# Two DMA queues instead of one in a hybrid decoder layer

## The chip, the cores and the metric

The kernel runs on one core of a Trainium2 chip. The metric is the device time of one execution in microseconds (us). The core has five engines that run side by side, each in its own order: PE (TensorE, matrix products), DVE (VectorE), ACT (ScalarE), POOL (GpSimd) and SP (SyncE). A transfer between memory (HBM) and the core's SBUF is issued by an instruction of SP, ACT or POOL; each of these issues its instructions in order, and if one of them has to wait (for data, or for a buffer to come free), all behind it wait too. This is what "queue" means below.

## The reference

One layer of a decoder, in float32, over 16 learned meta tokens and 2048 tokens of width 1024:

```python
h = jnp.concatenate([meta, x], axis=1)
for l in range(DEPTH):                       # DEPTH = 1
    u = _rmsnorm(h, mix_norm_g[l])
    p = u @ w_in[l]                          # 1024 -> 1792
    p_pool, p_bval, p_bgate, p_cgate, p_cx = jnp.split(p, splits, axis=-1)
    y_a = _pool_mixer(p_pool, pool_w[l], pool_scale[l])
    y_b = _conformer_conv(p_bval, p_bgate, ...)      # 31-tap causal convolution, layernorm
    y_c = _rglru_branch(p_cgate, p_cx, ...)          # gates, linear recurrence over time
    y = jnp.concatenate([y_a, y_b, y_c], axis=-1)
    h = h + y @ w_out[l]
    u = _rmsnorm(h, mlp_norm_g[l])
    h = h + jnp.square(jax.nn.relu(u @ w_up[l])) @ w_down[l]     # 1024 -> 4096 -> 1024
h = _rmsnorm(h, final_norm_g)
return h[:, N_META:]
```

## The kernel before, in words

**Precision.** Products are made in a reduced float format. Each operand is split into a high part and a low part (`split`, lines 113 and 114: ACT rounds to the high part, DVE subtracts to get the low one), and each product is three matmuls: high times high, high times low, low times high. So every weight tile has to be split before PE can use it, unless its split was stored earlier.

**Chunks and items.** The tokens are worked on in four chunks of 512 (chunk 0 has the 16 meta tokens as well). All of PE's large work is a list of items, made in advance: W (input projection, 14 blocks per chunk), O (output projection, 8 per chunk), U and D (up and down projection of the MLP, in four groups), and B (down projection with fewer products, chunk 3). In chunks 1 to 3 U uses a scheme of Strassen's kind: seven products of half size instead of eight, for which sums of weight blocks are needed. In order, O and W of one chunk stand between D of the chunk before and U of the next: O of chunk 1 follows D of chunk 0, and W of chunk 2 follows that.

**Side work.** Everything else (normalisation, mixers, the loads of activations, sums of weights) is written as Python generators. After each item `pump` advances them by a budget of estimated ns, so their instructions are strewn among the items. A scheduler of the framework then lays down the order on each engine and all waits.

**Weights.** The class `Weights` (from line 270 on) feeds the items in order. Raw tiles (128 x 512) are loaded into six buffers `wr` (line 151, called from `dma`), split into five buffers `wh` of twice the size (`split`), and used by PE. Where a split will be needed again, it is stored to HBM (line 309: `wk` for W, `ok` for O, `uk` for U of chunk 1), and later chunks load the stored split straight into `wh` (line 305) instead of splitting again. A `wh` buffer comes free when PE has used it and, if it is stored, when the store has landed.

**Transfers that the change touches**, all in SP's queue before:

- line 177, `gen_fold`: stores of a folded part of `w_out` (8);
- lines 204 to 214, `gen_sums`: loads of blocks of `w_up` into buffers `s` and `t`, sums on DVE, stores to `sums` (16 units of 4 loads and 4 stores), during chunk 0;
- lines 221 to 229, `gen_dsums`: the same for `w_down`, with a split; its high parts go through the `xr` buffers (12 units of 4 loads and 8 stores), during chunks 1 and 2;
- line 309: stores of splits (28 for W, 16 for O, 64 for U);
- line 468, `gen_x`: loads of the activations of chunks 1 to 3, eight each, through the `xr` buffers; line 483, `gen_late`, eight again for chunk 1;
- line 775, `evac_o`: loads of the old activations that O adds to its product, eight per chunk, also through `xr`; the addition is line 777, and it frees one of four PSUM buffers `pm`;
- line 1020, `gen_final`: stores of the results, eight per chunk 0 to 2 (chunk 3 has its own rule and keeps it).

There are two `xr` buffers for all of lines 228, 468, 483 and 775.

`gen_x` for chunk 2 runs during O of chunk 1, and that for chunk 3 during O of chunk 2, each behind `gen_final` of the chunk two before it: first a column sum on PE (lines 382 and 383, `colsum`) and a reciprocal (line 392), then eight scalings (line 1019) with eight stores, then eight loads with squares and splits (lines 400, 401, 158, 159), then a column sum of their squares.

The loads of raw weights are called with the queue as a default, which the change leaves alone:

```python
def w_raw(src, tag="xr", bufs=2, queue=nc.sync):
```

Of the kernel before, what the change touches and what calls it, by code (L numbers as in the profile page):

```python
# [25 lines left out]
F32 = mybir.dt.float32  # L26
# [8 lines left out]
NCH = 4  # L35
META = 16
W0 = NT + META
# [45 lines left out]
def build(nc, tc, x0, xr, w_in, w_out, w_fold, w_up, w_down, vecs, gates, pools, pws, out):  # L83
# [18 lines left out]
    def t_(tag, cols, bufs, dt=F32):  # L102
        shape = [P] + (list(cols) if isinstance(cols, (list, tuple)) else [cols])
        return sb.tile(shape, dt, name=nm(tag), tag=tag, bufs=bufs)
# [7 lines left out]
    def split(hi, lo, src):  # L112
        A.activation(out=hi, in_=src, func=AF.Copy)  # L113
        V.tensor_tensor(out=lo, in0=src, in1=hi.bitcast(F32), op=ALU.subtract)  # L114
# [18 lines left out]
    for b, (w0, w1) in enumerate(((2, 4), (8, 16))):  # L133
# [8 lines left out]
    d_kept = {  # L142
        (g, v): [dp.tile([P, 2, 512], F32, name=f"dk_{g}_{v}_{q}", tag=f"dk_{g}_{v}_{q}") for q in range(4)]
        for g in range(FG - 1) for v in range(KB // 2)
    }
    sums = [dp.tile([P, 2048], F32, name=f"sums_{u}", tag=f"sums_{u}") for u in range(NU)]

    def w_raw(src, tag="xr", bufs=2, queue=nc.sync):
        n = src.shape[-1]
        t = t_(tag, 512, bufs)[:, :n]  # L150
        queue.dma_start(out=t, in_=src)
        return t
# [13 lines left out]
    def gen_fold():  # L166

        pl, pw = b_tile(), b_tile()
        r1, r2 = w_raw(pools), w_raw(pws)
        split(pl[:, 0, :256], pl[:, 1, :256], r1)  # L170
        split(pw[:, 0, :512], pw[:, 1, :512], r2)
        yield 1300

        def store(ps, k, nh):
            t = t_("s", W0, SBF)[:, :NT]
            A.activation(out=t, in_=ps, func=AF.Copy)
            nc.sync.dma_start(
                out=wo_fold[nh * 4 : nh * 4 + 4, :, k * P : (k + 1) * P].rearrange("j p c -> p j c"),
                in_=t.rearrange("p (j c) -> p j c", j=4),
            )  # L180

        for nh in range(2):
            for b in range(2):
                w = f_tile(w_raw(w_fold[b][:, nh * 512 : nh * 512 + 512]), vc("psc", b))
                ps = ps_back()
                mm3(ps, [(pl[:, 0, b * P : (b + 1) * P], pl[:, 1, b * P : (b + 1) * P], w[:, 0], w[:, 1])])
                store(ps, b, nh)
                yield 750
            pss = [ps_back() for _ in range(2)]
            for j in range(2):  # L190
                w = f_tile(w_raw(w_fold[2 + j][:, nh * 512 : nh * 512 + 512]))
                for i in range(2):
                    m0 = j * 256 + i * P
                    mm3(pss[i], [(pw[:, 0, m0 : m0 + P], pw[:, 1, m0 : m0 + P], w[:, 0], w[:, 1])], j == 0, j == 1)
                yield 700
            for i in range(2):
                store(pss[i], 2 + i, nh)
            yield 0

    def gen_sums(u):  # L200

        a11, a12, a21, a22 = (t_(t, W0, n)[:, :512] for t, n in (("s", SBF), ("t", TB), ("t", TB), ("s", SBF)))
        for t, m, c0 in ((a21, 1, 0), (a22, 1, 512), (a11, 0, 0), (a12, 0, 512)):
            nc.sync.dma_start(out=t, in_=w_up[2 * u + m][:, c0 : c0 + 512])
        yield 0
        V.tensor_tensor(out=a22, in0=a21, in1=a22, op=ALU.add)
        V.tensor_tensor(out=a21, in0=a11, in1=a21, op=ALU.subtract)
        nc.sync.dma_start(out=sums[u][:, 1536:2048], in_=a22)
        nc.sync.dma_start(out=sums[u][:, 1024:1536], in_=a21)
        yield 1400  # L210
        V.tensor_tensor(out=a11, in0=a22, in1=a11, op=ALU.subtract)
        V.tensor_tensor(out=a12, in0=a12, in1=a11, op=ALU.subtract)
        nc.sync.dma_start(out=sums[u][:, 0:512], in_=a11)
        nc.sync.dma_start(out=sums[u][:, 512:1024], in_=a12)
        yield 1400

    def gen_dsums(g, v):

        a11, a12, a21, a22 = (t_(t, W0, n)[:, :512] for t, n in (("s", SBF), ("t", TB), ("t", TB), ("s", SBF)))
        for t, m, c0 in ((a21, 1, 0), (a22, 1, 512), (a11, 0, 0), (a12, 0, 512)):  # L220
            nc.sync.dma_start(out=t, in_=w_down[g, 2 * v + m][:, c0 : c0 + 512])
        yield 0

        def put(q, t):
            hi = t_("xr", NT, 2, F32R)
            A.activation(out=hi, in_=t, func=AF.Copy)
            V.tensor_tensor(out=t, in0=t, in1=hi.bitcast(F32), op=ALU.subtract)
            nc.sync.dma_start(out=d_kept[g, v][q][:, 0], in_=hi.bitcast(F32))
            nc.sync.dma_start(out=d_kept[g, v][q][:, 1], in_=t)

        V.tensor_tensor(out=a22, in0=a21, in1=a22, op=ALU.add)
        V.tensor_tensor(out=a21, in0=a11, in1=a21, op=ALU.subtract)
        yield 1400
        V.tensor_tensor(out=a11, in0=a22, in1=a11, op=ALU.subtract)
        V.tensor_tensor(out=a12, in0=a12, in1=a11, op=ALU.subtract)
        yield 1400
        put(0, a11)
        put(1, a22)
        yield 1400
        put(2, a21)  # L240
        put(3, a12)
        yield 1400
# [37 lines left out]
    class Weights:  # L280
# [17 lines left out]
        def split(self, n):  # L298
            while self.ns < min(n, len(self.srcs)):
                self.dma(self.ns + 1)  # L300
                t = t_("wh", (2, 512), WH, F32R)
                _, keep, kept = self.srcs[self.ns]
                with tc.high_priority(EARLY):
                    if kept is not None:
                        nc.sync.dma_start(out=t.bitcast(F32), in_=kept)
                    else:
                        split(t[:, 0], t[:, 1], self.raw.pop(self.ns))
                if keep is not None:
                    nc.sync.dma_start(out=keep, in_=t.bitcast(F32))
                self.hl[self.ns] = t  # L310
                self.ns += 1

# [95 lines left out]
    for c in range(NCH):  # L408
        o = Chunk()
# [15 lines left out]
    def a_tile():  # L425
        return t_("U", (2, NT), 8, F32R)

    def b_tile():
        return t_("H", (2, W0), HB, F32R)
# [30 lines left out]
    def gen_x(o):  # L460

        o.x = []
        if o.c > 1:
            ss = t_("ss", W0, 2)
        for k in range(KB):
            hl = a_tile()
            raw = t_("xr", NT, 2)
            nc.sync.dma_start(out=raw, in_=xr[o.c - 1, k])
            if o.c > 1:
                add_square(ss, raw, 0, NT, k == 0)  # L470
            split_to(hl[:, 0], hl[:, 1], raw, vc("g1", k))
            o.x.append(hl)
            yield 1300
        if o.c > 1:
            o.rs1 = rsqrt_of([colsum(ss[:, :NT])], subs_of(o), 1.0 / D)
            yield 3500

    def gen_late(o):

        ss = t_("ss", W0, 2)  # L480
        for k in range(KB):
            raw = t_("xr", NT, 2)
            nc.sync.dma_start(out=raw, in_=xr[o.c - 1, k])
            add_square(ss, raw, 0, NT, k == 0)
            yield 620
        o.rs1 = rsqrt_of([colsum(ss[:, :NT])], subs_of(o), 1.0 / D)
        yield 3500
        for kind, i, t in o.held:
            evac_w(o, kind, i, [t])
            yield 700  # L490
# [279 lines left out]
    def evac_o(o, j, ps):  # L770
        if j == 0:
            o.h = []
            o.ss2 = t_("ss", W0, 2)
        raw = t_("xr", NT, 2)
        nc.sync.dma_start(out=raw, in_=(x0[j, :, META:W0] if o.c == 0 else xr[o.c - 1, j]))
        h = htile(o, j)
        V.tensor_tensor(out=h[:, :NT], in0=ps, in1=raw, op=ALU.add)  # L777
        add_square(o.ss2, h[:, :NT], 0, NT, j == 0)
        o.h.append(h)
# [227 lines left out]
    def gen_final(o, s0, s1):  # L1007
        if o.c == NCH - 1:

            ps = ps_back()  # L1010
            for n, t in enumerate((o.ssf, o.sq7)):
                T.matmul(ps[:, : s1 - s0], ones.bitcast(F32), t[:, s0:s1], start=(n == 0), stop=(n == 1))
        else:
            ps = colsum(o.ssf[:, s0:s1])
        rs = rsqrt_of([ps], [(s0, s1)], 1.0 / D)
        yield 3300
        for k in range(KB):
            h = o.h[k][:, s0:s1]
            V.scalar_tensor_tensor(out=h, in0=h, scalar=vc("gf", k), in1=rs[:, s0:s1], op0=ALU.mult, op1=ALU.mult)
            (nc.scalar if o.c == NCH - 1 and k % 2 else nc.sync).dma_start(out=out[o.c, k, :, s0:s1], in_=h)  # L1020
            yield 660


# [113 lines left out]
    for it in items:  # L1137
        kind, c, j, _ = it
# [18 lines left out]
    for n, it in enumerate(items):  # L1157
        kind, c, j, (s0, s1) = it
        o = ch[c]
# [156 lines left out]
```

## Time and profile before

| | |
|---|---|
| Time, median of 3 runs | 2005.56 us (2005.14 to 2010.1) |
| The profiled execution | 2004.47 us |
| Its span, first to last instruction | 2002.6 us |
| Granted clock of PE, mean | 0.991 |
| DMA, all queues | 464.20 MB, mean 232 GB/s |
| q1, SP's queue | 199632 packets, 460.61 MB, 68.4% of 16 engines' span |
| q10, ACT's queue | 1584 packets, 1.64 MB, 0.2% |

The table says that practically all bytes went through SP's queue, and that the 16 DMA engines of the core were busy with it for about two thirds of the span. The profile's page cuts the span into 40 slices and gives a digit for the busy share of each engine, in tenths. The digits of PE are 9 nearly everywhere. An engine that is busy in nearly every slice sets the time, so the places where it is not busy are what one looks for; the waits, in which the profile says what each engine waited for and what ended the wait, tell why. In the lines of these views, `h<-pm,xr` is the output buffer and the inputs, and `SPq L1020` is an instruction that SP issues for line 1020. In the timeline the first number is the start in us from the start of the span, the second the duration, and the bracket tells how long the engine had been idle and what released it.

### The profile page before, as it was taken

To read this page: it belongs to the slowest core of one execution; us is meant where nothing else is said; L and a number is where in the kernel's file an instruction comes from. 1 tells how busy PE (TensorE), PEld (TensorE's weight loads), DVE (VectorE), ACT (ScalarE), POOL (GpSimd) and SP (SyncE) were. 2 spreads that over 40 slices of the span, in tenths; PEclk is the share of its full clock that TensorE was granted. 3 is DMA by queue.
4 is the path that set the end of the run, shared out by engine and by line. 5 is a ranking of instruction groups with operands and counts; after the bars stand their busy time and mean duration, and the time that the engine had idled before them with its cause. 6 is when DMAs were issued, how large, how long until landed. Compare 5 with 4: busy or idle time off the path is not lost.

```text
span 2002.6 us, 30672 instructions
## 1 busy us (share of the span) xinstructions
PE 1933.2 (97%) x11080; PEld 1672.0 (83%) x11080; DVE 1461.2 (73%) x2394; ACT 1016.6 (51%) x1704; POOL 0.2 (0%) x4
## 2 busy tenths in 40 slices
PE   8999999999999899999999889999999998999998
PEld 8778878777887689888888768988888888999998
DVE  7987589966753699569787489856768478676667
ACT  5586364556542326467675231545467435353443
POOL 0000000000000000000000000000000000000000
PEclk9999999999999899999999999999999999999999
DMA  9635756735847579488767759847876638888874
GB/s 319 206 127 192 246 178 197 239 121 180 267 151 246 179 249 320 137 300 282 256 236 258 247 184 307 293 156 271 301 255 212 228 116 281 285 279 283 282 253 153
DMA packets 201368, 464.20 MB, mean 232 GB/s; under 512 B 22144, under 2 KB 28416, under 8 KB 201216
## 3 DMA queue, kind: packets, MB, share of 16 engines
q1 hardware_dynamic: 199632, 460.61, 68.4%
q8 instruction: 87, 1.43, 0.3%
q10 hardware_dynamic: 1584, 1.64, 0.2%
q14 instruction: 65, 0.53, 0.1%
HBM read 353.11 MB, written 109.05 MB: 231 GB/s over the span
## 4 chain that ended last, share of the span: by engine, by line
PE 72%; DMA 12%; DVE 9%; ACT 4%; issue 3%; SPq 1%; ACTq 0%; DVEq 0%
PE pm L331 44%; PE pm L355 10%; PE pw L355 10%; PE pm L345 5%; DMA wh<-uk 3%; DMA xr<-d_xr 2%; DVE wh L114 2%; DVE ca L591 2%; DMA wh<-dk 1%; DMA uk<-wh 1%; ACT wh L113 1%; DMA s<-d_w_up 1%; PE pb L638 1%; DVE fr L870 1%; DMA t<-d_w_up 1%
## 5 line engine op out<-in xcount | busy, mean ns | idle before, releaser
L331 PE MATMUL pm<-U,wh 128*128 128x512 f32 (+1 forms) x3072 | 691.4, 384 | 5.7 <-DVE wh L114 5.5
L331 PEld LDWEIGHTS pm<-U,wh 128*128 128x128 f32 x3072 | 554.1, 188 | 131.5 <-DVE wh L114 6.6
L113 ACT ACTIVATE wh<-wr 128x512 fp32r<-128x512 f32 x576 | 355.4, 626 | 416.0 <-PE pm L331 227.3
L114 DVE TENSOR_TENSOR wh<-wr,wh 128x512 fp32r<-128x512 f32 x576 | 388.3, 687 | 184.3 <-ACT wh L113 180.2
L331 PE MATMUL pm<-H,wh 128*128 128x512 f32 (+1 forms) x2112 | 455.1, 374 | 22.4 <-DVE h L777 15.2
L331 PEld LDWEIGHTS pm<-H,wh 128*128 128x128 f32 x2112 | 373.3, 192 | 99.9 <-DVE h L777 16.9
L355 PE MATMUL pm<-H,wh 128*128 128x256 f32 x2304 | 293.5, 282 | 7.9 <-DMA wh<-uk 7.8
L355 PEld LDWEIGHTS pm<-H,wh 128*128 128x128 f32 x2304 | 282.2, 188 | 12.5 <-DMA wh<-uk 8.0
L355 PE MATMUL pw<-H,wh 128*128 128x256 f32 x1728 | 224.8, 283 | 11.0 <-DVE fr L870 6.6
L355 PEld LDWEIGHTS pw<-H,wh 128*128 128x128 f32 x1728 | 212.1, 189 | 17.2 <-issue 6.9
L345 PE MATMUL pm<-U,wh 128*128 128x512 f32 (+1 forms) x624 | 143.1, 387 | 0.1
L345 PEld LDWEIGHTS pm<-U,wh 128*128 128x128 f32 x624 | 113.2, 188 | 25.7 <-ACT wh L113 1.0
L591 DVE SCALAR_TENSOR_TENSOR ca<-Pbv,vec,ca 128x512 f32<-128x512 f32 x180 | 128.1, 745 | 0.1
L401 DVE TENSOR_TENSOR ss<-ss,fr 128x512 f32<-128x512 f32 (+1 forms) x82 | 53.4, 651 | 64.6 <-ACT fr L400 62.8
L870 DVE TENSOR_TENSOR fr<-pw,fr 128x512 f32<-128x512 f32 x96 | 66.1, 688 | 31.4 <-PE pw L355 29.4
L857 DVE TENSOR_TENSOR U<-fr,U 128x512 fp32r<-128x512 f32 x104 | 71.3, 687 | 21.3 <-ACT fr L856 21.0
L997 DVE TENSOR_TENSOR h<-h,pm 128x512 f32<-128x512 f32 (+1 forms) x100 | 66.8, 670 | 17.0 <-PE pm L331 15.8
L966 ACT ACTIVATE fr<-fr 128x512 f32<-128x512 f32 x48 | 30.2, 629 | 78.0 <-DVE fr L965 78.0
L400 ACT ACTIVATE fr<-h 128x512 f32<-128x512 f32 (+1 forms) x45 | 27.7, 620 | 77.4 <-DVE h L777 52.7
L855 ACT ACTIVATE U<-fr 128x512 fp32r<-128x512 f32 x104 | 64.9, 626 | 1.6
L856 ACT ACTIVATE fr<-fr 128x512 f32<-128x512 f32 x104 | 64.7, 624 | 1.4
L392 DVE RECIPROCAL rs<-rs 128x512 f32<-128x512 f32 (+2 forms) x17 | 53.9, 3169 | 13.5 <-ACT rs L390 13.4
(269 smaller groups left out, 1662.8 us busy)
## 6 DMA issues: line engine op xcount, KB each, us to landing
wr<-d_w_down SPq DMA_DIRECT2D x260, 256.0 KB, 3.6
wh<-uk SPq DMA_DIRECT2D x128, 512.0 KB, 5.2
wr<-d_w_up SPq DMA_DIRECT2D x208, 256.0 KB, 3.5
wh<-wk SPq DMA_DIRECT2D x64, 512.0 KB, 3.9
uk<-wh SPq DMA_DIRECT2D x64, 512.0 KB, 4.9
wh<-ok SPq DMA_DIRECT2D x48, 512.0 KB, 4.2
wh<-dk SPq DMA_DIRECT2D x48, 512.0 KB, 5.1
wr<-sums SPq DMA_DIRECT2D x64, 256.0 KB, 5.9
```

What stands on the lines that cost most here:

```text
L113: A.activation(out=hi, in_=src, func=AF.Copy)
L114: V.tensor_tensor(out=lo, in0=src, in1=hi.bitcast(F32), op=ALU.subtract)
L331: T.matmul(ps[:, : s1 - s0], w_block(w, k, a, paired), rhs[k][:, b, s0:s1], start=(k == 0 and j == 0), stop=(k == KB - 1 and j == 2),)
L345: T.matmul(ps[:, : s1 - s0], w_block(w, k, a, True), rhs[k][:, b, s0:s1], start=(k == 0 and j == 0), stop=(k == KB - 1 and j == 2),)
L355: T.matmul(ps, w[:, a, k * P : (k + 1) * P], op[k][b], start=(k == 0 and j == 0), stop=(k == 3 and j == 2),)
L392: V.reciprocal(rs[:, c0:c1], rs[:, c0:c1])
L591: V.scalar_tensor_tensor(out=a, in0=o.ub[i][:, k : k + NT], scalar=vc("cw", i * CONVK + k), in1=a, op0=ALU.mult, op1=ALU.add)
L855: A.activation(out=f[:, 0], in_=r, func=AF.Square)
L856: A.activation(out=r, in_=r, func=AF.Square)
L857: V.tensor_tensor(out=f[:, 1], in0=r, in1=f[:, 0].bitcast(F32), op=ALU.subtract)
L870: V.tensor_tensor(out=out.rearrange("p (a c) -> p a c", a=2), in0=ps.rearrange("p (a c) -> p a c", a=2), in1=x.unsqueeze(1).broadcast_to([ ...
L997: V.tensor_tensor(out=h, in0=h, in1=ps[:, : s1 - s0], op=ALU.add)
```

## The change

The listed transfers are issued by POOL (`nc.gpsimd`) instead of SP. SP keeps the first loads of the activations of chunk 0, the loads of raw weights and of stored splits, and half of the results of chunk 3; the other half of those stays on ACT. Nothing else changes: sizes, buffers, items and budgets are the same. The diff, without the lines around:

```diff
 gen_fold, store
-            nc.sync.dma_start(
+            nc.gpsimd.dma_start(
                 out=wo_fold[nh * 4 : nh * 4 + 4, :, k * P : (k + 1) * P].rearrange("j p c -> p j c"),
 gen_sums
-            nc.sync.dma_start(out=t, in_=w_up[2 * u + m][:, c0 : c0 + 512])
+            nc.gpsimd.dma_start(out=t, in_=w_up[2 * u + m][:, c0 : c0 + 512])
-        nc.sync.dma_start(out=sums[u][:, 1536:2048], in_=a22)
-        nc.sync.dma_start(out=sums[u][:, 1024:1536], in_=a21)
+        nc.gpsimd.dma_start(out=sums[u][:, 1536:2048], in_=a22)
+        nc.gpsimd.dma_start(out=sums[u][:, 1024:1536], in_=a21)
-        nc.sync.dma_start(out=sums[u][:, 0:512], in_=a11)
-        nc.sync.dma_start(out=sums[u][:, 512:1024], in_=a12)
+        nc.gpsimd.dma_start(out=sums[u][:, 0:512], in_=a11)
+        nc.gpsimd.dma_start(out=sums[u][:, 512:1024], in_=a12)
 gen_dsums
-            nc.sync.dma_start(out=t, in_=w_down[g, 2 * v + m][:, c0 : c0 + 512])
+            nc.gpsimd.dma_start(out=t, in_=w_down[g, 2 * v + m][:, c0 : c0 + 512])
-            nc.sync.dma_start(out=d_kept[g, v][q][:, 0], in_=hi.bitcast(F32))
-            nc.sync.dma_start(out=d_kept[g, v][q][:, 1], in_=t)
+            nc.gpsimd.dma_start(out=d_kept[g, v][q][:, 0], in_=hi.bitcast(F32))
+            nc.gpsimd.dma_start(out=d_kept[g, v][q][:, 1], in_=t)
 Weights.split
-                    nc.sync.dma_start(out=keep, in_=t.bitcast(F32))
+                    nc.gpsimd.dma_start(out=keep, in_=t.bitcast(F32))
 gen_x and gen_late
-            nc.sync.dma_start(out=raw, in_=xr[o.c - 1, k])
+            nc.gpsimd.dma_start(out=raw, in_=xr[o.c - 1, k])
 evac_o
-        nc.sync.dma_start(out=raw, in_=(x0[j, :, META:W0] if o.c == 0 else xr[o.c - 1, j]))
+        nc.gpsimd.dma_start(out=raw, in_=(x0[j, :, META:W0] if o.c == 0 else xr[o.c - 1, j]))
 gen_final
-            (nc.scalar if o.c == NCH - 1 and k % 2 else nc.sync).dma_start(out=out[o.c, k, :, s0:s1], in_=h)
+            ((nc.scalar if k % 2 else nc.sync) if o.c == NCH - 1 else nc.gpsimd).dma_start(out=out[o.c, k, :, s0:s1], in_=h)
```

More of the change, by code (lines that the diff above doesn't have):

```diff
@@ L482, in gen_late @@
             raw = t_("xr", NT, 2)
-            nc.sync.dma_start(out=raw, in_=xr[o.c - 1, k])
+            nc.gpsimd.dma_start(out=raw, in_=xr[o.c - 1, k])
             add_square(ss, raw, 0, NT, k == 0)
```

## The prediction, made before the result was known

> **What bounds the kernel now.** I read the page first, for the engine that fills the span.
>
> ```profile
> span 2002.6 us, 30672 instructions
> PE 1933.2 (97%) x11080; PEld 1672.0 (83%) x11080; DVE 1461.2 (73%) x2394; ACT 1016.6 (51%) x1704; POOL 0.2 (0%) x4
> PE 72%; DMA 12%; DVE 9%; ACT 4%; issue 3%; SPq 1%; ACTq 0%; DVEq 0%
> ```
>
> TensorE (PE) is busy for 1933.2 of 2002.6 us, so about 69 us of holes, and some slow matmuls behind them, are all that a change of transfers alone can win. GpSimd (POOL) does nothing after four start-up instructions. The second view is the list of waits of PE: it names what ended the holes.
>
> ```profile
> PE pm L331 <- DVE h L777: 15.2, 4, 5.9
> PE pb L382 <- ACT hl L113: 9.1, 4, 6.3
> PE pm L355 <- DMA wh<-uk: 7.8, 9, 1.9
> ```
>
> (Columns: total us, times, longest.) L777 is the addition that empties PSUM in the output projection (kind O); it needs the old activations in an `xr` buffer. L382 is the sum over columns, whose place in PE's order is fixed, so everything behind it waits as well. The third line is late weights. Third, the table by stretches, to see where the first two lie.
>
> ```profile
> 650.00:700.00 50.00, 39.89 (x152) 31.03 (x153) 34.01 (x52) 18.27 (x28) 0.00 (x0) 0.86 0.56 180
> 1150.00:1200.00 50.00, 43.77 (x174) 34.03 (x174) 41.23 (x64) 18.90 (x31) 0.00 (x0) 0.91 0.51 174
> ```
>
> After the length of the stretch comes PE's busy time. These two stretches, the projections of chunks 1 and 2, lose 10.1 and 6.2 us, and the granted clock falls to 0.86 and 0.91. The DMA share is only 0.56 and 0.51, so it is not bandwidth that lacks there. Fourth, the waits of the DMA queue on SyncE (SP), which issues in order.
>
> ```profile
> SPq L309 <- DVE wh L114: 150.1, 78, 11.0
> SPq L228 <- ACT xr L226: 31.5, 19, 6.0
> SPq L1020 <- DVE h L1019: 18.6, 7, 15.4
> ```
>
> All three lines are stores for whose data the queue stands still, with weights and activations behind them. These waits go away from SP with the change; most of them cost PE nothing, as DVE and the weights run ahead.
>
> **The first place: output projection of chunk 1.** The queue's view, then the timeline of the engines:
>
> ```profile
> 625.84 0.34 SPq L1020 DMA_DIRECT2D d_out<-h  x1
> 638.20 1.31 SPq L1020 DMA_DIRECT2D d_out<-h  x1
> 640.56 0.33 SPq L305 DMA_DIRECT2D wh<-ok  x1
> 640.98 0.87 SPq L468 DMA_DIRECT2D xr<-d_xr  x2
> ```
>
> ```profile
> 629.71 0.74 DVE L1019 SCALAR_TENSOR_TENSOR h<-h,vec,rs 128x512 f32<-128x512 f32 x1
> 630.97 0.74 DVE L159 SCALAR_TENSOR_TENSOR U<-xr,vec,U 128x512 fp32r<-128x512 f32 x1
> 645.80 0.63 ACT L400 ACTIVATE fr<-xr 128x512 f32<-128x512 f32 x1 [14.08 <-DMA xr<-d_xr]
> 653.31 7.83 PE L331 MATMUL pm<-H,wh 128*128 128x512 f32 x24 [4.42 <-DVE h L777]
> 667.41 0.79 PE L382 MATMUL pb<-hl,ones 128*128 128x512 f32 x1 [6.27 <-ACT hl L113]
> ```
>
> The eight results of chunk 0 (L1020) are ready when DVE ends the last one, 629.71 + 0.74 = 630.45. SP needs from 625.84 to past 638.20 for their stores, because between them stand loads `wh<-ok`, each of which waits until PE has released a weight buffer. Only then, at 640.98, come the next two loads of activations for chunk 2 (L468), though an `xr` buffer was free at 630.97 + 0.74 = 631.71. ACT waits 14.08 us for them. There are two `xr` buffers for eight such loads and for the additions at L777, so from 640.98 to the column sum at 667.41 run four rounds of load and use, 26.4 us. PE idles 4.42 and 6.27 us in it.
>
> With the change the eight stores and these loads stand in POOL's queue, in the same order among themselves, without the weights. Let g be POOL's time to issue one transfer, and d how much later than from SP it lands. Then the pair is issued at the later of 631.71 and 625.84 + 8g instead of 640.98, and the column sum comes 4d later for its four rounds: a change of 8g - 15.1 + 4d.
>
> **The second place: output projection of chunk 2.**
>
> ```profile
> 1116.68 5.38 DVE L1019 SCALAR_TENSOR_TENSOR h<-h,vec,rs 128x512 f32<-128x512 f32 x8
> 1117.65 0.42 SPq L1020 DMA_DIRECT2D d_out<-h  x1
> 1121.97 0.69 DVE L777 TENSOR_TENSOR h<-pm,xr 128x512 f32<-128x512 f32 x1
> 1131.28 0.45 SPq L1020 DMA_DIRECT2D d_out<-h  x1
> 1134.05 0.44 SPq L468 DMA_DIRECT2D xr<-d_xr  x1
> ```
>
> ```profile
> 1147.80 8.03 PE L331 MATMUL pm<-H,wh 128*128 128x512 f32 x24 [5.87 <-DVE h L777]
> 1157.12 0.51 PE L382 MATMUL pb<-hl,ones 128*128 128x512 f32 x1 [1.30 <-ACT hl L113]
> 1163.05 2.50 PE L331 MATMUL pm<-H,wh 128*128 128x512 f32 x5 [4.71 <-DVE h L777]
> ```
>
> The same figure: data ready at 1116.68 + 5.38 = 1122.06, stores from 1117.65, next load at 1134.05; PE idles 5.87 + 1.30 + 4.71 = 11.9 us. The last hole ends behind a fifth round (the addition after the column sum). In POOL's queue the load goes at 1117.65 + 8g, and both buffers are free from 1121.97 + 0.69 = 1122.66. Change: 8g - 16.4 + 5d.
>
> **The third place: results of chunk 2 between the weights of chunk 3.**
>
> ```profile
> 1668.32 1.93 SPq L1020 DMA_DIRECT2D d_out<-h  x2
> 1680.08 0.71 PE L355 MATMUL pm<-H,wh 128*128 128x256 f32 x4 [1.93 <-DMA wh<-uk]
> ```
>
> SP stands 1.93 us at these stores, loads `wh<-uk` behind it, and PE later waits 1.93 us for such a load. I credit that once: -1.9 us. The other late weights of the third line of PE's waits lie where no moved transfer stands ahead of them, or can't be told apart; I credit nothing, and 7.8 - 1.9 = 5.9 us is what it could be at most.
>
> **What POOL's queue adds.** The program moves 476 transfers: 8 of the fold, 16 x 8 of the sums of `w_up`, 12 x 12 of those of `w_down`, 108 stored splits (28 + 16 + 64), 64 loads of activations, 24 results. None of them was issued by POOL in this trace, so g and d have to be bounded. For g: SP's rows above show 0.34 to 0.45 us for an issue; at the other end POOL would issue one only when the one before has landed, 3.4 us:
>
> ```profile
> xr<-d_xr SPq DMA_DIRECT2D x56, 256.0 KB, 3.4
> xr<-d_gates SPq DMA_DIRECT2D x1, 256.0 KB, 2.8
> ```
>
> For d: the same size landed in 2.8 us where little else was queued, so a transfer that no longer queues behind weights may gain 0.6; and it can lose a whole landing, 3.4. In total even 476 x 3.4 = 1618 us fits into the span, so POOL as a whole is not full; only its places count. I take g = 0.8, twice SP's row, as the same 128 rows have to be described, and d = 0.5, near zero for the same DMA engines.
>
> Where d hurts is where a store has to land before its buffer can be used again:
>
> ```profile
> ACT wh L113 <- DMA uk<-wh: 11.7, 8, 2.9
> ACT xr L226 <- DMA dk<-xr: 23.1, 15, 4.5
> ```
>
> ```profile
> 854.26 0.63 ACT L113 ACTIVATE wh<-wr 128x512 fp32r<-128x512 f32 x1 [2.79 <-DMA uk<-wh]
> 863.08 1.67 PE L355 MATMUL pw<-H,wh 128*128 128x256 f32 x12 [2.02 <-DVE fr L870]
> ```
>
> ```profile
> 381.34 11.32 PE L345 MATMUL pm<-U,wh 128*128 128x512 f32 x48
> 386.97 0.82 ACT L623 ACTIVATE t<-Pcx,vec 128x512 f32<-128x512 f32 x1 [2.98 <-DMA sums<-t]
> 397.66 4.62 PE L331 MATMUL pm<-U,wh 128*128 128x512 f32 x12 [3.84 <-DVE wh L114]
> ```
>
> In the U blocks of chunk 1 ACT already waits 8 times for a stored split to leave its `wh` buffer; the wait of 2.79 us at 854.26 is followed by a hole of 2.02 us on PE. I let all eight grow by d and reach PE: 8d. The stores of the sums of `w_up` did the same once (2.98 us of ACT, then 3.84 us of PE); two of them: 2d. The 15 waits for `dk<-xr` I cost at nothing: they lie in the D blocks, where 48 matmuls, two items or four weight tiles, take 11.32 us, so the five tiles prepared ahead cover some 14 us against a longest wait of 4.5; without that cover they would cost another 15d. SP's issue time that falls away lies beside PE's work and is worth nothing by itself.
>
> **The sum.** 8g - 15.1 + 4d, and 8g - 16.4 + 5d, and -1.9, and 10d make 16g + 19d - 33.4. With g = 0.8 and d = 0.5: -6.7, -7.5, -1.9 and +5.0, together -11.1 us. The profiled execution took 2004.47 us (span 2002.6 and 1.9 around it); it becomes 1993.4. The median of the runs before, 2005.56, is 1.1 above the profiled execution, so I forecast 1994.5 us. Late next on PE would still be the column sum, about 6 us earlier than now.
>
> The Trainium skill, page "DMA: Bandwidth & Descriptors", section "Latency and other measured facts", gives about 0.6 us to the first byte from SyncE and about 1 us from GpSimd, where software writes the descriptors; no run here shows it yet. By it d would be 0.4, and the sum, as an estimate, -13.0 instead of -11.1 us.
>
> **Rivals.** *No change.* The change does not do all that it says: the loads of activations still stand behind the eight result stores, only in another queue, and the two `xr` buffers still make four or five rounds in turn. At g = 1.0 and d = 0.9 the sum is 16.0 + 17.1 - 33.4 = -0.3: 2005.3 us. For it speak the rounds in the rows above, against it that d would be a quarter of a whole landing, 0.9 of 3.4. The same page's section "Issuing engines are not separate DMA queues" speaks for it, too: transfers of all queues run on the same DMA engines, and another queue saves only issue time. The trace agrees that bandwidth is not missing in the two stretches (DMA shares 0.56 and 0.51), but what SP loses there is waiting in line, not issue time.
>
> *Slower.* POOL's transfers are dear enough to turn every round and every buffer that a store has to leave into a longer wait. It decides from 16g + 19d = 33.4 on. At g = 1.5 and d = 1.5 the stores take 12 us before the load can go, the two projections end 2.9 and 3.1 us later than now, the stored splits and sums cost 15, and the third place still gives 1.9 back: 24.0 + 28.5 - 33.4 = +19.1, 2024.7 us. For it: ACT's waits of 11.7 us show that the split buffers have no slack in chunk 1. Against it: g there would be four times SP's row.
>
> *Much faster.* g = 0.4 and d = -0.6: the load goes as soon as its buffers are free, and the holes of both projections close, 10.7 + 11.9 us; the 24 matmuls after each, which took 7.83 and 8.03 us where 48 take 11.32, run 2.2 us faster each; with the third place -29 us, 1977 us. Against it: the rounds through two buffers would have to become shorter than PE's work.
>
> **How the numbers follow.** A measurement of this kernel can tell about 0.3%, 6 us, from no change. The sum is faster than that when 16g + 19d is below 27.4 (at g = 0.8, d below 0.77), slower when it is above 39.4 (at g = 0.8, d above 1.4). I give 0.39 to the forecast, 0.08 to much faster, 0.27 to no change and 0.26 to slower: 0.47 faster, 0.27 same, 0.26 slower. The range for 8 in 10 reaches from near the much faster case, 1978, to near the slower one, 2022. By itself the forecast's own range is 1985 to 1999.
>
> **What would show it.** Right: POOL issues of under 1 us; the load L468 after the last L1020 at about 7 us (chunk 1) and 10 us (chunk 2) sooner after the first L1020 than now; PE's wait at L777 nearly gone, that at L382 shorter; clock above 0.9 in those stretches; ACT's waits for `uk<-wh` up by a few us. Wrong: landings from POOL over 1 us later than from SP, more of PE's time waiting for `wh` splits in chunk 1, new holes in the D blocks of chunk 0 behind `sums`, or an order of instructions on PE that moves the column sum to another place, which I have left as it is.

## The result, and the profile after

In the runs on one chip the kernel before took 2005.35 us (median of 4), the kernel after 2102.05 us (median of 4): 1.0468 times as long, 95% interval 1.044 to 1.0497. The profiled execution of after took 2094.55 us, its span is 2092.8. I had forecast 1994.5; the sign was wrong. The top of the page of after:

```profile
span 2092.8 us, 30923 instructions
PE 1959.3 (94%) x11080; PEld 1695.1 (81%) x11080; DVE 1463.3 (70%) x2394; ACT 1014.7 (48%) x1702; POOL 259.6 (12%) x480
...
q1 hardware_dynamic: 128016, 307.49, 45.4%
q0 software_dynamic: 44992, 153.12, 20.2%
```

The change did what it says: 153 MB moved to a queue of POOL (q0), and POOL is busy 12% of the span, with issuing. PE does the same 11080 matmuls. Its holes grew from 69 to 133 us (span less busy time), and the matmuls themselves took 26 us more, at a mean granted clock of 0.976 instead of 0.991. The two prices that the prediction had bounded can be read from the groups and from the landings of after:

```profile
L309 POOL DMA_DIRECT2D uk<-wh x64 | 34.2, 534 | 269.1 <-DVE wh L114 205.8 <-DVE fr L965 62.7 <-issue 0.2
...
uk<-wh POOLq DMA_DIRECT2D x64, 512.0 KB, 5.7
xr<-d_xr POOLq DMA_DIRECT2D x56, 256.0 KB, 4.0
dk<-xr POOLq DMA_DIRECT2D x48, 256.0 KB, 4.5
```

An issue takes 534 ns here and 0.54 us as the mean of all 480 (259.6 us), so g = 0.54, under my 0.8. The landings were 4.9, 3.4 and 3.4 us before: by these medians d is 0.6 to 1.1, say 0.85, over my 0.5. In the formula of the prediction they give 16 x 0.54 + 19 x 0.85 - 33.4 = -8.6 us. (It is -6.4 us if the loads also have to wait for their buffers, free at 631.71 and 1122.66; the formula had left that bound out, which counts at so low a g.) So it isn't the medians of the two prices that failed, but the formula.

The first place, the output projection of chunk 1, in the timeline of after:

```profile
654.92 5.18 POOL L1020 DMA_DIRECT2D d_out<-h  x8 [3.50 <-DVE h L1019]
660.79 1.18 POOL L468 DMA_DIRECT2D xr<-d_xr  x2 [0.69 <-DMA d_out<-h]
668.02 0.63 ACT L400 ACTIVATE fr<-xr 128x512 f32<-128x512 f32 x1 [7.60 <-DMA xr<-d_xr]
678.07 4.44 PE L331 MATMUL pm<-H,wh 128*128 128x512 f32 x18 [0.47 <-DVE h L777]
690.57 0.79 PE L382 MATMUL pb<-hl,ones 128*128 128x512 f32 x1 [8.06 <-ACT hl L113]
```

The loads L468 go 660.79 - 654.92 = 5.9 us after the first result, where it was 640.98 - 625.84 = 15.1. The wait at L777 is down to 0.47 us. The column sum comes 35.7 us after the first result instead of 41.6: 5.9 us won, where the terms of this place, 8g - 15.1 + 4d, give -7.4 at the measured prices, and -5.9 with the bound by the buffer. PE gained less: from the first matmul of this output projection to the first of the next stage it took 57.4 us, 61.0 before, as the wait ahead of the column sum grew from 6.27 to 8.06 us. The second output projection took 56.3 us, 62.4 before. So both places gained. In the table by stretches they lie at 650 to 700 and 1200 to 1250; a third stretch is worse, at the head of the U blocks of chunk 2. The same work had PE busy for 47.92 us (364 matmuls, clock 1.00) in the stretch 1250 to 1300 of before:

```profile
650.00:700.00 50.00, 41.47 (x166) 32.81 (x166) 29.30 (x37) 14.93 (x24) 11.90 (x22) 0.90 0.73 246
...
1200.00:1250.00 50.00, 40.46 (x166) 31.95 (x165) 34.97 (x54) 17.17 (x26) 4.85 (x9) 0.90 0.59 189
1300.00:1350.00 50.00, 38.68 (x264) 36.50 (x263) 42.53 (x68) 15.73 (x28) 7.06 (x13) 0.86 0.77 260
```

So the time is lost elsewhere. The waits of PE say at what:

```profile
PE pw L355 <- DVE fr L870: 36.7, 16, 6.5
PE pb L382 <- ACT hl L113: 20.1, 4, 8.6
PE pm L355 <- DMA wh<-uk: 12.4, 9, 3.9
```

The same wait as in the first line, before:

```profile
PE pw L355 <- DVE fr L870: 6.6, 9, 2.0
```

Here PE waits for DVE to add up the results in `pw`. The second line, the wait at the column sum, which I had expected to be shorter, was 9.1 us before. One of the 16 times of the first line, in a U block of chunk 2, with what DVE and ACT did ahead of it:

```profile
1313.02 2.93 PE L355 MATMUL pm<-H,wh 128*128 128x256 f32 x12 [3.88 <-DMA wh<-uk]
1314.37 0.63 ACT L226 ACTIVATE xr<-t 128x512 fp32r<-128x512 f32 x1 [6.09 <-DMA dk<-xr]
1320.06 3.39 DVE L591 SCALAR_TENSOR_TENSOR ca<-Pbv,vec,ca 128x512 f32<-128x512 f32 x5
1323.97 0.69 DVE L870 TENSOR_TENSOR fr<-pm,q 128x512 f32<-128x512 f32 x1
1327.10 0.69 DVE L870 TENSOR_TENSOR fr<-pw,fr 128x512 f32<-128x512 f32 x1
1327.84 2.93 PE L355 MATMUL pw<-H,wh 128*128 128x256 f32 x12 [6.48 <-DVE fr L870]
```

Two things stand here. ACT waits 6.09 us for a store of a weight sum to land. And DVE, which is not idle, runs seven taps of the convolution (L591) and three splits of weights (L114) in the 7 us before the addition that PE needs, at 1327.10. The taps are this place's own: in all 16 waits together they fill 4.0 of the 36.7 us, splits of weights 12.1, and for 8.3 DVE stands idle until ACT has done its half of a split (L113). What stands ahead of what on DVE is a matter of order: the framework lays the instructions of each engine out by its own model of time, and with another queue it laid them out anew. If one compares the two programs engine by engine and keeps as many instructions as possible that stand in the same order in both, 154 of PE's 11060 are left over, 486 of DVE's 2394 and 211 of ACT's 1655.

### The profile page after: what moved, and what is told of

It is laid out like the page before. It is cut to its first block, busy times and chain, and to the rows that moved or that the text cites. A ratio compares the mean times of both kernels' runs of the same rounds, so it can differ in the third digit from the quotient of the medians.

```text
span 2092.8 us, 30923 instructions
## 1 busy us (share of the span) xinstructions
PE 1959.3 (94%) x11080; PEld 1695.1 (81%) x11080; DVE 1463.3 (70%) x2394; ACT 1014.7 (48%) x1702; POOL 259.6 (12%) x480
## 4 chain that ended last, share of the span: by engine, by line
PE 44%; issue 22%; DMA 16%; DVE 10%; POOL 4%; ACT 3%; POOLq 0%; DVEq 0%; ACTq 0%; SPq 0%
PE pm L331 25%; PE pm L355 7%; PE pw L355 7%; PE pm L345 3%; DMA xr<-d_xr 3%; DVE ca L591 3%; DMA wh<-uk 2%; DMA s<-d_w_up 2%; DMA wh<-dk 2%; DVE wh L114 1%; DMA uk<-wh 1%; POOL uk L309 1%; DMA sums<-s 1%; DMA dk<-t 1%; DMA dk<-xr 1%
## 5 line engine op out<-in xcount | busy, mean ns | idle before, releaser
L113 ACT ACTIVATE wh<-wr 128x512 fp32r<-128x512 f32 x576 | 356.5, 627 | 452.0 <-PE pm L331 244.1
L114 DVE TENSOR_TENSOR wh<-wr,wh 128x512 fp32r<-128x512 f32 x576 | 390.3, 688 | 237.5 <-ACT wh L113 235.1
L331 PEld LDWEIGHTS pm<-H,wh 128*128 128x128 f32 x2112 | 374.8, 193 | 91.8 <-ACT wh L113 7.2
L355 PE MATMUL pm<-H,wh 128*128 128x256 f32 x2304 | 301.6, 287 | 14.4 <-DMA wh<-uk 12.4
L355 PEld LDWEIGHTS pm<-H,wh 128*128 128x128 f32 x2304 | 291.0, 194 | 19.1 <-DMA wh<-uk 11.8
L355 PE MATMUL pw<-H,wh 128*128 128x256 f32 x1728 | 235.3, 291 | 50.6 <-DVE fr L870 36.7
L355 PEld LDWEIGHTS pw<-H,wh 128*128 128x128 f32 x1728 | 221.1, 196 | 58.4 <-issue 29.2
L591 DVE SCALAR_TENSOR_TENSOR ca<-Pbv,vec,ca 128x512 f32<-128x512 f32 x180 | 128.5, 750 | 0.1
L870 DVE TENSOR_TENSOR fr<-pw,fr 128x512 f32<-128x512 f32 x96 | 66.1, 688 | 28.2 <-PE pw L355 26.4
L309 POOL DMA_DIRECT2D uk<-wh x64 | 34.2, 534 | 269.1 <-DVE wh L114 205.8
```

What stands on the lines that cost most here:

```text
L309: nc.gpsimd.dma_start(out=keep, in_=t.bitcast(F32))
L331: T.matmul(ps[:, : s1 - s0], w_block(w, k, a, paired), rhs[k][:, b, s0:s1], start=(k == 0 and j == 0), stop=(k == KB - 1 and j == 2),)
L355: T.matmul(ps, w[:, a, k * P : (k + 1) * P], op[k][b], start=(k == 0 and j == 0), stop=(k == 3 and j == 2),)
L591: V.scalar_tensor_tensor(out=a, in0=o.ub[i][:, k : k + NT], scalar=vc("cw", i * CONVK + k), in1=a, op0=ALU.mult, op1=ALU.add)
L870: V.tensor_tensor(out=out.rearrange("p (a c) -> p a c", a=2), in0=ps.rearrange("p (a c) -> p a c", a=2), in1=x.unsqueeze(1).broadcast_to([ ...
```

## The experiments

**Theories.** *Order*: the new order of PE, DVE and ACT costs the time, whatever the queue. *Transfer*: what POOL issues lands later, and buffers and engines wait for it. To part them I held the order. A table for each engine lists one kernel's instructions in their order, and each instruction gets an edge to the one before it that binds the order of issue alone:

```diff
+    for text in ORDERS.values():
+        ...
+            tc.add_manual_dep(
+                ins, prev.name,
+                mybir.DependencyInfo(mybir.DependencyClass.NoSync, mybir.DependencyReason.DATA),
```

The kernel before, held to its own order in this way, is the same program, instruction for instruction, so the edges add nothing. "Old order" below means that PE, DVE, ACT and SP are held to the order of before. The tables shift the line numbers: by 75 in the kernels at old order, by 86 in the two with small writes.

**Order and queue apart.** `e1`: the diff of the change, at the old order. `e2`: before, with PE, DVE and ACT held to the order of after.

> All moved transfers are issued by POOL as in the changed kernel, but the order of instructions on PE, DVE, ACT, SP and (among the moved ones) POOL is pinned to that of the kernel before, by edges that order issue only. Theory 'order' (the framework's scheduler, which works with its own model of time, laid down another order on DVE, ACT and PE because the queue changed, and that order costs the 90 us): the loss is gone, about 1997 us (the sum of the prediction with the measured issue of 0.54 us and 0.85 us later landing: -8.6), at any rate 1985 to 2015. Theory 'transfer' (POOL's transfers land later and stand in one line, so buffers of splits and sums come free later): as slow as the changed kernel, 2080 to 2105.

> All transfers stay in SP's queue as before, but the order of instructions on PE, DVE and ACT is pinned to that of the changed kernel. Theory 'order': as slow as the changed kernel, 2070 to 2110. Theory 'transfer': like the kernel before, 2000 to 2015.

| kernel | queue | order | median, us | to before (95%) |
|---|---|---|---|---|
| after | POOL | new | 2102.05 | 1.0468 (1.044 to 1.0497) |
| `e1` | POOL | old | 2054.04 | 1.0247 (1.0215 to 1.028) |
| `e2` | SP | new | 2109.46 | 1.0532 (1.05 to 1.0565) |

The kernel before took 2002.75 us beside `e1` and `e2`. Neither theory is alone. The transfers cost 51 us without a change of order, and on top of them the new order costs 48 us (after against `e1`). The order of after costs 107 us even without a single transfer moved. The two don't add: at the new order the POOL queue is no worse than SP's. Part of the 107 us is a mismatch, as a place of `e2` shows (its line numbers are 59 higher than before's: L290 is L231, L929 is L870):

```profile
1528.07 0.69 DVE L290 TENSOR_TENSOR s<-t,s 128x512 f32<-128x512 f32 x1 [10.99 <-DMA s<-d_w_down]
1528.68 0.68 DVE L929 TENSOR_TENSOR fr<-pw,fr 128x512 f32<-128x512 f32 x1
1529.42 4.44 PE L414 MATMUL pw<-H,wh 128*128 128x256 f32 x24 [6.44 <-DVE fr L929]
```

DVE stands idle for 10.99 us until blocks of `w_down` have landed for a weight sum, and the addition that PE needs stands behind. Its waits for these blocks are 69 us in all, 14 before and 22 in after. So this order suits loads that don't stand in line behind weights, and the price of the order in after itself is the 48 us.

**The groups of transfers, order free and held.** The edit is the diff of the change, for the lines named alone: activations and results (468, 483, 775, 1020), stored splits (309), sums and fold (177, 204 to 229).

> Only the loads of activations (lines 468, 483, 775) and the results (line 1020) go to POOL; stored splits, sums and the fold stay on SP; the scheduler is free. Theory 'transfer': the terms for stored splits and sums fall away, and the two output projections gain as in the prediction, 16 x 0.54 + 9 x 0.85 - 33.4 = -17, 1988 us (1980 to 2000). Theory 'order': the order changes here too, so part of the loss stays although no stored split is on POOL, 2010 to 2070.

> Only the stores of splits (line 309) go to POOL, the scheduler is free. Theory 'transfer': these stores hold the weight buffers of chunk 1 longer, where the changed kernel lost some 30 us in the U blocks of chunk 1, so 2020 to 2045. Theory 'order': the loss follows what the scheduler does with the order, not the buffers; waits of ACT for these stores stay near the 11.7 us of before, and holes of PE end at DVE instead.

> Only the weight sums and the fold (lines 177, 204 to 229) in GpSimd's queue, the order laid anew. If 'order' and 'transfer' add, the transfers give what this group gives at the old order (next run, about 1.018) and the order something between 0 and 25 us more: 1.018 to 1.030. If the new order happens to suit, no more than 1.018.

> Order of the engines that of the kernel before; only lines 468, 483, 775 and 1020 (activations and results of the last norm) in GpSimd's queue. With all but the splits it was 42 us slower at this order. Theory 'sums' (those 42 us belong to the weight sums and their results: store, landing, next use of the same two buffers xr and of t, with ScalarE standing in line): 0.993 to 1.000 here, the gains at the heads of chunks 1 and 2 alone. Theory 'any transfer from GpSimd' (each group pays for landing later): 1.005 to 1.012, the gains eaten.

> Order of the engines that of the kernel before; of the transfers only the stored splits (line 309) go to GpSimd's queue, all others stay in SyncE's. Theory 'split buffer' (what is left of the loss at the old order, some 50 us, is that the five buffers of the weight splits are given back later, because each store is issued and lands later from GpSimd: 34 us of ScalarE's waits for uk<-wh, 11.7 before): 1.015 to 1.025 of the time before, with those waits at 25 us or more. Theory 'sums and results' (the loss sits with the sums of chunk 2, whose results land later, 33.9 us of waits for dk<-xr against 23.1): 1.000 to 1.005.

> The same group at the order of before. All but the splits cost 42 us at this order and the activations 5 of them: 1.016 to 1.021, with the place of 12 us in the D stage of chunk 2. If the groups only hurt together (activations and sums in one line on GpSimd), under 1.010.

> Order of the engines that of the kernel before; all of the change except line 309: activations, results, sums and fold in GpSimd's queue, stored splits in SyncE's. 'Split buffer': 0.994 to 1.003, the place of 15 us in the D stage of chunk 2 gone or nearly so, and the gain at the heads of chunks 1 and 2 kept (2 to 5 us each). 'Sums and results': 1.015 to 1.025, with the place in chunk 2 still there.

| moved to POOL | order free | old order |
|---|---|---|
| activations, results | `e3` 1.0027 (1.0008 to 1.0046) | `e10` 1.0024 (1.0003 to 1.0045) |
| stored splits | `e4` 1.0221 (1.0187 to 1.0255) | `e6` 1.0109 (1.0088 to 1.0131) |
| sums, fold | `e5` 1.0325 (1.03 to 1.0351) | `e17` 1.0211 (1.0171 to 1.0251) |
| all but the splits | | `e7` 1.02 (1.0157 to 1.0243) |
| all | after 1.0468 | `e1` 1.0247 |

A new order isn't dear as such: with the activations it leaves out 102 instructions of PE, and costs nothing beyond the transfers; with the splits and with the sums it costs some 22 us each, all together 48. At the old order the sums alone cost the 42 us that I had laid to all but the splits, the splits 22, and these don't add up either (51 us for all). `e7` came where "sums and results" had it; `e6` fell between the two, as the splits cost more than that theory allowed and less than the other. For the activations neither case came: no gain, and half the loss of the other. The activations, for which the whole gain was forecast, cost 5 us (1 to 9 by the interval of `e10`). At the first place of `e10` the timeline shows why:

```profile
632.33 3.19 POOL L1095 DMA_DIRECT2D d_out<-h  x5 [3.51 <-DVE h L1094]
635.90 1.83 POOL L1095 DMA_DIRECT2D d_out<-h  x3 [0.38 <-DVE h L1094]
638.48 1.19 POOL L543 DMA_DIRECT2D xr<-d_xr  x2 [0.75 <-DMA d_out<-h]
646.79 0.63 ACT L475 ACTIVATE fr<-xr 128x512 f32<-128x512 f32 x1 [8.95 <-DMA xr<-d_xr]
670.89 0.80 PE L457 MATMUL pb<-hl,ones 128*128 128x512 f32 x1 [6.44 <-ACT hl L188]
```

The loads go 6.2 us after the first result, 9.0 sooner than before. But eight results in a row and SP's weights are in flight ahead of them, so the first needs 646.79 - 638.48 = 8.3 us until ACT can use it, where it was 645.80 - 640.98 = 4.8. The column sum comes 38.6 us after the first result, 3.0 less than before, and the whole output projection takes 60.1 us, 0.9 less. At the second place the load goes 5.6 us after the first result, 10.8 sooner than before, and gains nothing:

```profile
1125.62 0.54 POOL L543 DMA_DIRECT2D xr<-d_xr  x1
1135.59 0.63 ACT L475 ACTIVATE fr<-xr 128x512 f32<-128x512 f32 x1 [10.05 <-DMA xr<-d_xr]
```

It needs 10.0 us until ACT can use it, 4.7 before. The column sum comes 39.1 us after the first result, 39.5 before, and the output projection takes 62.9 us, 62.4 before. The table by stretches of before, cut to these two places, tells the reason (the last but one column is the DMA share):

```profile
625.00:646.00 21.00, 21.00 (x92) 16.99 (x91) 7.37 (x12) 2.08 (x4) 0.00 (x0) 1.00 0.97 317
1117.00:1138.00 21.00, 21.00 (x92) 17.05 (x91) 6.35 (x10) 1.58 (x3) 0.00 (x0) 1.00 0.91 302
```

Before the change the DMA engines were already busy for 0.97 and 0.91 of the time in which the load stood in line; in `e10` it is 0.95 (632 to 648) and 0.99 (1120 to 1136). A load that is issued sooner there waits beside the others instead of behind them.

**More buffers.** If a store that lands late matters because a buffer is given back late, one more buffer covers it.

```diff
 e8, e9
-                t = t_("wh", (2, 512), WH, F32R)
+                t = t_("wh", (2, 512), WH + 1, F32R)
-            sq = t_("fr", W0, FR)
+            sq = t_("fr", W0, FR - 1)
 e12, e13
-            hi = t_("xr", NT, 2, F32R)
+            hi = t_("xr", NT, 3, F32R)
```

(All other places of `fr` and `xr` likewise; `e8` and `e12` have the whole change, `e9` and `e13` the queue of before, all the old order. `e14` is `e9` with the activations and results on POOL.)

> The whole change at the old order, with a sixth buffer for the weight splits and three instead of four of the buffers fr that pay for it. 'Split buffer': within 1.005 of the same buffers with everything in SyncE's queue (its neighbour here), as the later return of one buffer is covered by the sixth. 'Sums and results', or a slower path of GpSimd's transfers as such: 1.02 to 1.03 of its neighbour, as at five buffers.

> The neighbour of the run before: six buffers of splits, three of fr, everything in SyncE's queue, old order. Both theories: 0.995 to 1.015 of the time before (a sixth buffer can help a little, the missing fr can cost); it is there for the comparison.

> The whole change at the old order, with three buffers xr in place of two (they hold the raw activations and the high halves of the sums until the store has landed). If ScalarE's wait for the landing of dk<-xr (33.9 us) is what the sums cost, 15 to 30 us of the 50 are gone against its neighbour with three buffers in SyncE's queue: 1.010 to 1.016 of it. If not, still 1.02 to 1.03 of it.

> The neighbour: three buffers xr, everything in SyncE's queue, old order. 0.99 to 1.00 of the time before, since the 23 us of ScalarE's waits for dk<-xr there mostly stand beside work of TensorE.

> Six buffers of weight splits and three fr at the old order (0.988 with everything in SyncE's queue), and the four lines of the first run here in GpSimd's queue. 'Sums': 0.982 to 0.988 of the time before. 'Any transfer from GpSimd': 0.992 to 1.000.

| buffers | all on SP | whole change | difference |
|---|---|---|---|
| as before | 2002.75 | `e1` 2054.04 | 51 us |
| six `wh`, three `fr` | `e9` 1977.66, 0.9882 (0.9858 to 0.9906) | `e8` 2022.0, 1.0095 (1.0069 to 1.0121) | 44 us |
| three `xr` | `e13` 1993.03, 0.9952 (0.9935 to 0.9969) | `e12` 2033.84, 1.0153 (1.0133 to 1.0174) | 41 us |

`e14` took 0.9907 (0.9876 to 0.9938). Both buffers help, but they help the kernel before, too: of the gap of 51 us they take 7 and 10, little more than the intervals leave open. So it is not mainly one scarce buffer, neither of splits nor of `xr`: both buffer theories fell. By the way `e9` beats both kernels: six split buffers, everything in SP's queue, 1.2% under before; `e14` shows no gain from the activations there either.

**Loads or stores of the sums.** Lines 204 and 221 alone (`e18`), or 208, 209, 213, 214, 228 and 229 alone (`e19`), at the old order.

> Old order; only the loads of the weight sums (lines 204 and 221) in GpSimd's queue, their stores in SyncE's, in line with the weights again. With loads, stores and the fold there it was 42 us slower. Theory 'late stores' (what costs is that a store lands later, and with it the next use of its buffer): 0.998 to 1.006. Theory 'late loads' (VectorE, which is in line for them, waits for s and t): 1.012 to 1.022.

> The counterpart: only the stores of the weight sums (lines 208, 209, 213, 214, 228 and 229) in GpSimd's queue, their loads in SyncE's. 'Late stores': 1.014 to 1.022, with the place of 12 us in the D stage of chunk 2. 'Late loads': 0.998 to 1.008.

`e18` took 1.009 (1.0065 to 1.0115), `e19` 1.0109 (1.0082 to 1.0136): 18 for the 112 loads and 22 us for the 160 stores, against 42 for both with the fold. Neither theory: each kind pays. A place of `e19` at which PE loses, at the head of a U block of chunk 2 (the expectations call it the D stage), in the timeline:

```profile
1434.29 4.96 SPq L226 DMA_DIRECT2D wr<-d_w_up  x2
1435.54 0.54 POOL L304 DMA_DIRECT2D dk<-t  x1 [0.67 <-DVE t L302]
1439.84 2.67 SPq L380 DMA_DIRECT2D wh<-uk  x3
1443.76 1.28 ACT L722 ACT_TABLE_LOAD   x1 [5.67 <-DMA dk<-t]
1447.39 5.46 PE L430 MATMUL pw<-H,wh 128*128 128x256 f32 x24 [4.18 <-DMA wh<-uk]
1448.51 0.69 DVE L729 SCALAR_TENSOR_TENSOR t<-t,t 128x512 f32<-128x512 f32 x1 [9.02 <-ACT t L727]
1457.91 2.90 PE L430 MATMUL pw<-H,wh 128*128 128x256 f32 x12 [3.35 <-DVE fr L945]
```

The same place of the kernel before:

```profile
1417.93 0.32 SPq L229 DMA_DIRECT2D dk<-t  x1
...
1420.23 1.28 ACT L647 ACT_TABLE_LOAD   x1
...
1424.98 0.69 DVE L654 SCALAR_TENSOR_TENSOR t<-t,t 128x512 f32<-128x512 f32 x1 [3.45 <-ACT t L652]
...
1431.18 3.10 PE L355 MATMUL pw<-H,wh 128*128 128x256 f32 x24 [1.06 <-DMA wh<-uk]
```

This is one chain from a store to PE. ACT's instruction L722 (L647 before) writes a buffer `t` from which a store has to have landed. Before, it goes 2.3 us after the store's issue without a wait; in `e19` 8.2 us after it, 5.67 of them waited: the store landed 2.0 us after its issue before, and 8.15 us in `e19`. DVE, in order, stands 9.02 us behind ACT, and the addition L945, which frees PSUM, stands behind that; PE loses 3.35 us there, after 4.18 at weights that are later, too. A landing that POOL makes 1 us later is not enough for that. What else differs is SP: it doesn't stand behind the stores any more and sends weights, 256 and 512 KB each, to land at the same time. That they are the reason is an argument so far; the next two runs try it.

**Do the weights overtake?** `e15` holds each transfer of SP until the transfers that stood ahead of it in the old queue have been issued by POOL; `e16` has the small writes that this takes, and not the waits.

```diff
+    def from_pool(**kw):
+        nc.gpsimd.dma_start(**kw)
+        nc.gpsimd.memset(tok[:1, len(tokens) : len(tokens) + 1], 0.0)
+    ...
+            if last is not None and ins.name not in tokens:
+                after(ins, last.name, True)
```

> The whole change at the old order, and each transfer of SyncE is held until the transfers that stood ahead of it in the old queue have been issued from GpSimd (a one-element write on GpSimd behind each of its transfers, on which SyncE waits). Theory 'overtaking' (the 50 us come from weights that no longer stand behind the stores: they run ahead, up to 11 transfers are in flight where 7 were, and stores land 7 to 9 us after their issue, where ScalarE and the buffers wait for them): 1.000 to 1.010 of the time before, stores of dk over 6 us back from 24 to under 12, at most 8 in flight. Theory 'path' (a transfer from GpSimd is later whatever stands beside it): 1.018 to 1.028, as without the wait.

> The same small writes on GpSimd, and no wait of SyncE for them: the control. Both theories: 1.022 to 1.030, as without the writes (1.0247), since GpSimd is idle for most of the time.

`e15` took 2030.21 us, 1.0139 (1.0116 to 1.0161), `e16` 2052.44, 1.0257 (1.0229 to 1.0285), before 2002.22 beside them. Neither theory alone, once more: holding the weights back takes 22 of the 50 us; 28 stay. They are not all the price of POOL's path, as the old places are restored on one side only: SP waits for POOL in `e15`, but POOL doesn't wait for SP, so its own transfers can still run ahead of weights, and SP's waits for the small writes are in the time as well. From the issue and landing of each transfer in the traces (in flight: issued and not yet landed):

| | before | `e16` | `e15` |
|---|---|---|---|
| transfers in flight when a `wh<-uk` is issued, most | 5 | 11 | 9 |
| of 96 stores `dk`, landed over 6 us after issue | 7 | 25 | 18 |
| of 108 stored splits, over 6 us | 20 | 39 | 27 |

The mean in flight is 2.7, 2.8 and 2.7: it is bursts that differ. In `e6`, where the stored splits alone are POOL's and at most 6 are in flight, 37 of the 108 splits land over 6 us after issue; so for them the weights that run ahead are not the whole cause. The waits of ACT in `e16` and then in `e15`: those for the splits fall by 10 us, those for the sums hardly.

```profile
ACT xr L312 <- DMA dk<-xr: 36.2, 16, 5.2
ACT wh L199 <- DMA uk<-wh: 25.8, 18, 3.1
```

```profile
ACT xr L312 <- DMA dk<-xr: 34.4, 18, 4.0
ACT wh L199 <- DMA uk<-wh: 15.5, 12, 2.6
```

## Why the prediction was wrong

- *The order.* The step that failed first is the sentence that I had left "an order of instructions on PE" as it is. All terms were worked out on the order of before. `e1` against after puts 48 us on that. I had named it, for PE alone, as what would make me wrong and given it no case and no chance. It is not PE's order alone: the wait that grew most is for DVE's additions (L870), 6.6 us before, 20.5 in `e1` and 36.7 in after.
- *The output projections.* 8g - 15.1 + 4d and 8g - 16.4 + 5d took a load that is issued sooner for one that lands sooner, with the same small d everywhere. At the order on which they were worked out, it didn't: in `e10` 9.0 us of earlier issue became 3.0 us at the first column sum, and 10.8 became 0.4 at the second. In place of d = 0.5 the first load of each place took 3.5 and 5.2 us longer than before. My "it is not bandwidth that lacks there" was a misreading: 0.56 and 0.51 are means over 50 us, and in the 21 us in which the loads stood in line the DMA share was 0.97 and 0.91, before anything was changed. That the first place of after won just the 5.9 us that the terms give with the buffer's bound is in part luck: its first load took 2.4 us longer (7.2 against 4.8), where 4d has 3.4 spread over four rounds, and its order was new, too. The Trainium skill, page "DMA: Bandwidth & Descriptors", section "Issuing engines are not separate DMA queues", says that the transfers of all issuers run on the same 16 engines and that another issuer saves only the issue time. I had set that aside for this place; the landings of 8.3 and 10.0 us agree with it, and the 9.0 us saved in the line were real but mostly not worth having.
- *The splits.* "Eight waits grow by d": 8d is 6.8 us at 0.85, but moving the splits alone cost 22 us at the old order. ACT's waits for `uk<-wh` went from 8 times and 11.7 us to 14 and 19.1 there (`e6`), and to 18 and 34.0 in after. At the old order it is more stores that are waited for, and not the same ones longer.
- *The sums.* 2d, and nothing for `dk` as 14 us of prepared tiles cover a wait of ACT. The sums cost 42 us. The 15 waits for `dk` were misread: only 8 of them lie in D blocks, 4 in U blocks and 3, the longest among them, in the input projections. And cover on one engine was the wrong count: ACT works in order, so what waits behind ACT is DVE, and behind DVE the addition that PE needs next, as the place in `e19` shows. Even the fallback price, 15d or 13 us, would have been too low.
- *d.* 0.85 is a median. Over 6 us after issue land 25 of the 96 stores `dk` in `e16` and 7 before, and the wait at the place of `e19` is for such a store. Part of the tail comes from the weights that run ahead: in `e15` it is 18. The Trainium skill, page "DMA: Bandwidth & Descriptors", section "Latency and other measured facts", gives times to the first byte that lie, as an estimate, some 0.4 us apart; the medians moved by 0.2 to 2.0 us from group to group, so by its figure alone the price would have been too low, too.
- *The rival on the slower side* came nearest, with buffers that a store leaves later, but it made this pay by dear issues (g = 1.5), and the issues were cheap; and one more buffer of either kind took only 7 and 10 of the 51 us. Its chance of 0.26 was given for another cause.

What stays open: why 28 us are left in `e15`. Later landings in many chains at once are the likeliest (0 to 1.5 us in the medians of its groups of transfers), but no run varied them alone, and none held POOL back behind SP. And which engine's new order costs the 48 us: no run held one engine alone.

## What to carry to other kernels

A transfer's queue is also a place in line: here a store in front of the weights kept them from filling the DMA engines ahead of it, and taking it out let them. Where a transfer stands in line, read the DMA share in just that stretch, not in a mean over 50 us: if the engines are full, another queue moves the wait and doesn't end it. Before moving a transfer, follow from its landing to the busiest engine through every engine that works in order, and price that chain, not the median landing. And where a framework lays out the order itself, a change of queue is a change of order; hold the order by edges to see the two apart.

## What the runs showed of the hardware

In after an issue took POOL 0.53 to 0.55 us for 256 and 512 KB alike (means by group; 0.76 for the eight stores of the fold), where the medians of SP's groups before were 0.32 to 0.48. No issue from POOL took over 0.78 us, though DVE was busy for 70% of the span, so there is no sign that DVE's work holds POOL's issues up. A transfer from POOL landed 0.2 to 2.0 us later by group medians. In a burst the queue made little difference: in `e19` those issued from 1433.7 to 1441.2 landed 6.1 to 8.6 us after issue, from either queue, at a DMA share of 0.97 (1434 to 1446). At the old order a sixth buffer of weight splits, paid for by one `fr`, was worth 1.2%.
